# Attention behind the recurrent mixer, and the first tile's sort behind the middle attention

## The chip, the core and the metric

One core of one Trainium2 chip runs the whole program. The metric is the device time of one execution in microseconds; the time before is 3634.22 us, the median of 3 runs (3633.6 to 3636.48). Engines: PE (TensorE, matmul), DVE (VectorE), ACT (ScalarE), POOL (GpSimd), SP (SyncE, which here only issues DMAs). Each takes its instructions in order.

## The reference

One layer of a diffusion backbone on 1024 latent and 256 context tokens of width 1024:

```
hl, hc = rmsnorm(x) * (1 + scale) + shift          # scale and shift from c, c_ctx
r, k, v, w, a, g | q, k, v | b, c, x = split(h @ w_in)
y = concat(rwkv7(r, k, v, w, a, g),                 # two directions, 4 heads, state carried along T
           neighbourhood_attention(q, k, v, ctx),   # 8 heads, window 8 rows x 16 columns, plus 256 context keys
           b * conv3(c * x))
x = x + g1 * (y @ w_out)
h2 = rmsnorm(x) * (1 + scale2) + shift2
q = h2 @ q_w                                        # 8 heads, two halves
idx, gates = softmax(top16 of sums of the top16 of q . sub_keys)
x = x + g2 * sum_k gates[k] * gelu(u[idx[k]] . h2) * v[idx[k]]
out = rmsnorm(x) * final_g
```

All of it is float32 to the outside; a large product is made of three products of a high and a low part (`mm3`, lines 159 to 161), after a cast of each operand to its high part on ScalarE and a subtraction for the low one.

## The kernel before, in words

Stages, by the time in the profiled execution:

- **Projections and mixer (to about 766 us).** `proj` makes 128 output features for a block of 256 or 512 tokens: weights loaded by SP, cast on ACT (L207), low part on POOL (L209), 24 products into a PSUM bank (`pj`), copied out and stored to DRAM. The mixer (`batch(step, d)`) handles 4 chunks of 64 tokens in direction d. It has a long chain: loads, `wr` products, tanh and exponentials on ACT, scans on DVE, products `p1`, `p2`, `tr`, `lkv` for each of two pairs of heads, a substitution of 15 steps on DVE (L575 to L577, result `XT`), products `x0`, `lp`, `lt`, `lx` twice, `x12`, `pr`, then 4 chunks of state steps (`mc`, `yc`, copy `M` on ACT). The second direction to reach a chunk adds both outputs, normalises them on DVE (`y`, `yd`, L674), turns them with the product `yo` and stores them to `d_y`.
- **Fillers.** `fill(BESIDE)` is called six times in a batch and takes work from the generator `others()` until the amount owed is used up. `others()` holds the remaining projections, the convolution (`conv`, on DVE, its tiles `cu`, `cz`, `cs` loaded and stored by SP), then the first attention (query tiles 0 and 1) and the middle attention (2 to 5).
- **Attention.** `attend` runs per head: loads of keys, queries and values from DRAM (`kd`, `qd`, `vN`), casts (`kh`, `qs` on ACT, `kl` on POOL, low half of `qs` on DVE, L728), then for each query tile the score products `pw` and `pc`, maxima on DVE, exponentials on ACT, transposes `pt`, copies, the product `po` and the scaling `yn` (L776). A pair "head, query tile" is called a tile of attention below; the first attention has 16, the middle one 32. The argument `tags` names the PSUM banks of `pw`, `pt`, `po` and `pc`: ra has 3 banks, rb 2, ch 1, pj 2.
- **Group 0 (tokens 0 to 255).** `group(0)`: 192 output products (`o`) of the mixers' results `d_y`, norm and transposes (`s2`, `xt`), 16 query products of 24 matmuls (`q`), each copied on ACT (`qh`, L923), multiplied with keys (`sc`, L926), copied (`so`) and searched on DVE (`top_keys`). `topk(0)` sorts the first tile on DVE, in two halves; its first step is a cast on ACT (`tf`, L952).
- **Group 1 (tokens 256 to 767)** follows, with row gathers on POOL and their sums on DVE beside it, then the dense expert stage, with which the program goes on to its end. The last attention (tiles 6 and 7) and group 2 run inside it.

What sets the order: the kernel is written in program order, and a scheduler orders each engine's instructions ahead of time by what was emitted first and what it takes to be ready then. On the chip each engine keeps this order, so that an instruction that waits holds all behind it. Tiles are recycled: a tile waits until the last reader of the one that had its space is done.

Of the kernel before, what the change touches and what calls it, by code (L numbers as in the profile page):

```python
# [40 lines left out]
PACE = dict(g0=5, g1=(40,), u=450)  # L41
# [7 lines left out]
EASED = (1, 5, 7)  # L49
LAST = (7, 0, 8, 1, 9, 2, 3, 4, 5, 6)  # L50
HP = (600, 500)
BESIDE = 1.4


@with_exitstack
def hybrid_kernel(ctx: ExitStack, tc: tile.TileContext, A: dict, out: bass.AP, dbg=None):
    nc = tc.nc
# [6 lines left out]
    def pool(name, bufs=1, side="left"):  # L64
        return tc.tile_pool(name=name, bufs=bufs, side=side, reuse_waits="tile")
# [106 lines left out]
    def drain(gen):  # L172
        for _ in gen:
            pass
# [17 lines left out]
    def load_h(t0, n, i):  # L192
        new_h((t0, n), i)
        for k2 in range(KD // 2):
            hf = WT[0].tile([P, 2, 512], F32, tag=WT[1][0], name=f"hf{k2}_{t0}{i}", bufs=NWB)[:, :, :n]
            nc.sync.dma_start(hf, d_h[:, 2 * k2:2 * k2 + 2, t0:t0 + n])
            for j in range(2):
                split_h(2 * k2 + j, hf[:, j, :], n)
# [178 lines left out]
    def conv_inputs(blk):  # L377
        for i in range(2):
            zc = stg(f"zc{i}{blk[0]}")
            yield proj(23 + i, blk, lambda ps, t0, n, zc=zc: nc.scalar.copy(zc, ps))  # L380

            def uev(ps, t0, n, i=i, zc=zc):
                ev = nc.vector.tensor_mul(zc, ps, zc)
                nc.sync.dma_start(d_u[:, i, t0 - TC:t0 - TC + n], zc)
                return ev

            yield proj(25 + i, blk, uev)
            yield proj(21 + i, blk, spill(d_zb[:, i, :], TC))

    def head_inputs(blk, na=0):  # L390
        for i in range(4):
            more_ada(na)
            yield proj(13 + i, blk, spill(d_kn[:, i, :]))
            yield proj(17 + i, blk, spill_tok(d_vn, i * P))
            if blk[0]:
                more_ada(na)
                yield proj(9 + i, blk, spill(d_q[:, i, :], TC, scale=0.125))
# [65 lines left out]
    def batch(step, d):  # L463
# [14 lines left out]
        for h in range(2):  # L478
# [83 lines left out]
            for u in range(4):  # L562
# [4 lines left out]
                        rx=rx, krd=krd, vS=vS, tot=tots, gt=gt)  # L567
            fill(BESIDE)

# [15 lines left out]
        nc.scalar.copy(X, v8(ps))  # L585
        fill(BESIDE)

        for l in range(2):
# [13 lines left out]
            nc.vector.tensor_add(XT, v8(ps), XT)  # L602
            fill(BESIDE)
        for h in range(2):
# [7 lines left out]
        for h in range(2):  # L612
# [7 lines left out]
            s["pr"] = pr  # L620
        fill(BESIDE)

# [76 lines left out]
                nc.sync.dma_start(d_y[:, 6 + i, t0:t1], s_)  # L699


    def attend(na, qbs, w0, w1, tags, nbuf):


        q0, nq, nk = qbs[0] * P, len(qbs) * P, TC + w1 - w0
        yns = [na.tile([P, 512], F32, tag=f"yn{i}", name=f"yn{qb}", bufs=1) for i, qb in enumerate(qbs)]
        ns = TC + (640 if any(4 <= 2 * qb <= 10 for qb in qbs) else 512)
        for hd in range(8):
            f, half = divmod(hd, 2)
            if not half:  # L710
                vN, fs = na.tile([P, nk // P, P], F32, tag="vN", name=f"vN{f}{q0}", bufs=2), slice(f * P, (f + 1) * P)
# [79 lines left out]
    def others():  # L791

        for blk, na, i in ((TBLK[2], 2, None), (TBLK[1], 1, 1), (TBLK[0], 2, 1)):
            if i is not None:
                load_h(*blk, i)
            for _ in itertools.chain(head_inputs(blk, na), conv_inputs(blk) if blk[0] else ()):
                yield blk[1] / 512
        st_w.close()
        nc.vector.tensor_add(modT[:, 16:, 0], modT[:, 16:, 0], ab[:, 16:])
        conv(0, 256)  # L800
        conv(256, TL)
        with pool("na", 2, "right") as na:
            for _ in attend(na, range(0, 2), 0, 512, ("ra", "pj", "pj", "ra"), (3, 2, 1, 2, 1)):
                yield 0.6
        with pool("nb1", 1, "right") as na:
            for _ in attend(na, range(2, 6), 0, 1024, ("ra", "pj", "pj", "ra"), (3, 2, 1, 1, 1)):
                yield 0.6

    rest, owed = others(), [None]

    def fill(n):

        if owed[0] is not None:
            owed[0] += n
            while owed[0] > 0:
                owed[0] -= next(rest, 100.0)
# [15 lines left out]

    st_k = ExitStack()
    tk = st_k.enter_context(pool("tk", 1, "right"))
    st_i = ExitStack()
    ip = st_i.enter_context(pool("ip"))
    idx = ip.tile([P, 8, P], I32, name="idx")
# [318 lines left out]
    def advance(n):  # L1156

        while done[0] < n:
            done[0] += 1
            next(gat, None)  # L1160
# [21 lines left out]
        gbase[0] = g0 + ng  # L1182

    with pool("tp") as tp_:
        for i, _ in enumerate(group(0, tp_, nc.vector)):
            if i == 15:
                drain(topk(0, 0, 4))
                advance(PACE["g0"])
        drain(topk(0, 4, 4))
    hb2 = st_u.enter_context(pool("hb2"))  # L1190
    hd_["h2"] = [hb2.tile([P, KD, TD], F32R, name=n_) for n_ in ("h2h", "h2l")]
    h2h, h2l = hd_["h2"]
# [7 lines left out]

    def last_tiles():
        with pool("nb", 2, "right") as na:
            yield from attend(na, range(6, 8), 512, 1024, ("ra", "rb", "ch", "ra"), (2, 2, 1, 2, 2))
        yield from range(REST[0])
        with pool("tp2", 1, "right") as tp_:
            for i, ev in enumerate(group(2, tp_, nc.vector)):
                if i % 2:
                    yield ev
                if i == 7:
                    yield from range(REST[1])  # L1210
# [15 lines left out]
    def operands(g, j):  # L1226
# [16 lines left out]
        vs.append((vh, vl))  # L1243

    rest, opened, onehot, gdone = last_tiles(), True, None, 0
    st_g = ExitStack()
    for e in range(P):
# [202 lines left out]
```

## Time and profile before

| | us |
|---|---|
| median of 3 runs | 3634.2 |
| profiled execution | 3638.1 |
| its span | 3636.1 |
| last projection's end | 766 |
| last product of the mixer (`yo`) | 1063 |
| first output product of group 0 | 1078 |
| last query product of group 0 | 1219 |
| first output product of group 1 | 1236 |

Reading: the page gives each engine's busy share; the times of the table are from the timeline of PE. A stage is a stretch between two of them, and busy time over length tells which engine fills it. The idle time of an engine says little before one knows what ended it.

### The profile page before, as it was taken

To read this page: it belongs to the slowest core of one execution; us is meant where nothing else is said; L and a number is where in the kernel's file an instruction comes from. 1 tells how busy PE (TensorE), PEld (TensorE's weight loads), DVE (VectorE), ACT (ScalarE), POOL (GpSimd) and SP (SyncE) were. 2 spreads that over 40 slices of the span, in tenths; PEclk is the share of its full clock that TensorE was granted. 3 is DMA by queue.
4 is the path that set the end of the run, shared out by engine and by line. 5 is a ranking of instruction groups with operands and counts; after the bars stand their busy time and mean duration, and the time that the engine had idled before them with its cause. 6 is when DMAs were issued, how large, how long until landed. Compare 5 with 4: busy or idle time off the path is not lost. (4 is left out here: it accounts for less than half of the span.)

```text
span 3636.1 us, 62360 instructions
## 1 busy us (share of the span) xinstructions
PE 3270.1 (90%) x23447; PEld 2910.8 (80%) x23447; DVE 2796.9 (77%) x6131; ACT 1515.4 (42%) x2921; POOL 1357.7 (37%) x1052
## 2 busy tenths in 40 slices
PE   7788899858798679899899999999987999999997
PEld 6566778657688558889899999999976788888885
DVE  6654444546666859898899999998868888888888
ACT  3543333225455333364335766666522333323322
POOL 3332233211110132554334335455544444444433
PEclk9899999979799889999999999999998999999998
DMA  7434444353345446999888779999899999999996
GB/s 253 138 100 140 140 133 138 110 149 89 87 117 167 156 154 205 333 311 346 271 294 284 266 277 360 340 369 368 325 354 371 361 350 349 357 350 342 354 348 236
DMA packets 404718, 926.39 MB, mean 255 GB/s; under 512 B 45504, under 2 KB 182080, under 8 KB 398784
## 3 DMA queue, kind: packets, MB, share of 16 engines
q1 hardware_dynamic: 246976, 406.71, 34.7%
q0 software_dynamic: 111920, 407.95, 31.0%
q10 hardware_dynamic: 45520, 107.76, 7.7%
q8 instruction: 184, 3.01, 0.3%
q14 instruction: 118, 0.97, 0.1%
HBM read 800.64 MB, written 121.63 MB: 254 GB/s over the span
## 5 line engine op out<-in xcount | busy, mean ns | idle before, releaser
L1119 POOL DMA_INDIRECT ru<-in_peer_u_dram,idx x384 | 516.5, 1345 | 700.9 <-ACT dqs L1353 155.1
L1119 POOL DMA_INDIRECT rv<-in_peer_v_dram,idx x384 | 502.1, 1307 | 663.7 <-ACT dqs L1353 186.4
L1147 DVE SCALAR_TENSOR_TENSOR acc<-rv,gw,acc 128x1024 f32<-128x1024 f32 x381 | 488.4, 1282 | 30.1 <-DMA rv<-in_peer_v_dram,idx 25.5
L1136 DVE CUSTOM_DVE_ANT_0 ru<-ru,h 128x1024 f32<-128x1024 f32 x384 | 463.6, 1223 | 42.2 <-DMA ru<-in_peer_u_dram,idx 41.9
L160 PE MATMUL dp<-dvls,dwhs 128*128 128x512 f32 x896 | 348.3, 391 | 0.0
L161 PE MATMUL dp<-dvhs,dwls 128*128 128x512 f32 x896 | 346.5, 391 | 0.0
L209 POOL TENSOR_TENSOR wl<-w,wh 128x1024 fp32r<-128x1024 f32 x68 | 165.3, 2433 | 385.1 <-ACT wh L207 372.5
L159 PE MATMUL dp<-dvhs,dwhs 128*128 128x512 f32 x896 | 247.5, 394 | 0.1
L159 PE MATMUL pj<-hbh,wh 128*128 128x512 f32 (+1 forms) x544 | 219.4, 404 | 26.0 <-ACT wh L207 12.2
L160 PE MATMUL pj<-hbl,wh 128*128 128x512 f32 (+1 forms) x544 | 213.5, 393 | 3.7 <-POOL hbl L190 3.7
L1268 ACT ACTIVATE ge<-ds 128x256 f32<-128x256 f32 (+1 forms) x256 | 110.7, 433 | 250.0 <-PE ds L161 235.1
L161 PE MATMUL pj<-hbh,wl 128*128 128x512 f32 (+1 forms) x544 | 211.6, 389 | 2.8 <-POOL wl L209 2.8
L159 PEld LDWEIGHTS dp<-dvhs,dwhs 128*128 128x128 f32 x896 | 170.8, 191 | 36.1 <-ACT dvhs L1234 0.6
L160 PEld LDWEIGHTS dp<-dvls,dwhs 128*128 128x128 f32 x896 | 169.7, 189 | 35.6
L161 PEld LDWEIGHTS dp<-dvhs,dwls 128*128 128x128 f32 x896 | 169.5, 189 | 35.6
L1238 ACT CAST dwhs<-dws 128x640 fp32r<-128x640 f32 x128 | 91.9, 731 | 238.0 <-DVE dws L1237 209.4
L159 PE MATMUL dq<-dvhs,dwhs 128*128 128x512 f32 x384 | 151.6, 395 | 33.0 <-ACT dvhs L1234 26.5
L1234 ACT CAST dvhs<-dvs 128x1024 fp32r<-128x1024 f32 x128 | 134.0, 1051 | 90.8 <-DMA dvs<-in_peer_v_dram 90.7
L207 ACT CAST wh<-w 128x1024 fp32r<-128x1024 f32 x68 | 71.1, 1046 | 233.8 <-PE pj L160 151.9
L1353 ACT COPY dqs<-dq 128x512 f32<-128x512 f32 x90 | 52.8, 587 | 277.1 <-PE dq L161 277.1
L1051 PE MATMUL gm<-oa,ob 128*128 128x128 f32 x1280 | 159.1, 277 | 4.0 <-DVE oa L1038 3.3
L1235 DVE TENSOR_TENSOR dvls<-dvs,dvhs 128x1024 fp32r<-128x1024 f32 x128 | 156.0, 1219 | 8.3 <-ACT dvhs L1234 8.1
(1980 smaller groups left out, 9975.1 us busy)
## 6 DMA issues: line engine op xcount, KB each, us to landing
du<-in_peer_ut_dram SPq DMA_DIRECT2D x128, 512.0 KB, 6.2
dvs<-in_peer_v_dram SPq DMA_DIRECT2D x128, 512.0 KB, 6.9
d_ge<-ge ACTq DMA_DIRECT2D x128, 320.0 KB, 5.5
d_g<-gt ACTq DMA_DIRECT2D x40, 1024.0 KB, 9.8
dgs<-d_g SPq DMA_DIRECT2D x32, 1280.0 KB, 8.9
dws<-d_ge SPq DMA_DIRECT2D x128, 320.0 KB, 8.9
w<-in_w_in_dram SPq DMA_DIRECT2D x68, 512.0 KB, 3.7
wq<-in_q_w_dram SPq DMA_DIRECT2D x48, 512.0 KB, 4.2
```

The lines of the kernel that those rows point to most:

```text
L159: nc.tensor.matmul(ps, lh_, rh_, start=start, stop=False)
L160: nc.tensor.matmul(ps, lh_, rl_, start=False, stop=False)
L161: nc.tensor.matmul(ps, ll_, rh_, start=False, stop=stop)
L209: WE[0].tensor_tensor(wl, w, wh.bitcast(F32), op=OP.subtract)
L1051: nc.tensor.matmul(ps[:, t * P:(t + 1) * P], ob[:, q + t], oa[:, q + t], start=True, stop=True)
L1119: paced(nc.gpsimd.indirect_dma_start(out=r, out_offset=None, in_=A[tab], in_offset=bass.IndirectOffsetOnAxis(ap=idx[:, tt, s:s + 1], axis=0)))
L1136: yield from rows("peer_u", tt, lambda s, u: nc.vector.tensor_tensor_reduce(u, u, h2, 1.0, 0.0, OP.mult, OP.add, act[:, s:s + 1]))
L1147: nc.vector.scalar_tensor_tensor(acc, v, w[:, s:s + 1], acc, op0=OP.mult, op1=OP.add)
L1234: nc.scalar.copy(vh, v)
L1235: sv = nc.vector.tensor_tensor(vl, v, vh.bitcast(F32), op=OP.subtract)
L1238: nc.scalar.copy(wh, wt)
L1268: ev = nc.scalar.activation(ge[:, t0:t0 + n], ps, AF.Gelu_apprx_tanh)
```

## The change

Four edits. `BESIDE` goes from 1.4 to 1.2. Both attentions leave `others()`: the first is emitted behind the last batch of the mixer, with all four roles on the bank tag pj for heads 0 to 3 and ra, pj, ch, ra from head 4 on (so `tags` becomes a function of the head); the middle one, now with ch instead of pj for `po`, is emitted behind group 0. The sort of tile 0 is one piece instead of two halves, behind the middle attention; the first five steps of the gathers (`advance`) follow it as before. Computation and data are the same.

```diff
-BESIDE = 1.4
+BESIDE = 1.2
...
-    def attend(na, qbs, w0, w1, tags, nbuf):
+    def attend(na, qbs, w0, w1, tags_, nbuf):
...
         for hd in range(8):
+            tags = tags_(hd)
...
         conv(256, TL)
-        with pool("na", 2, "right") as na:
-            for _ in attend(na, range(0, 2), 0, 512, ("ra", "pj", "pj", "ra"), (3, 2, 1, 2, 1)):
-                yield 0.6
-        with pool("nb1", 1, "right") as na:
-            for _ in attend(na, range(2, 6), 0, 1024, ("ra", "pj", "pj", "ra"), (3, 2, 1, 1, 1)):
-                yield 0.6
...
     tk = st_k.enter_context(pool("tk", 1, "right"))
+    with pool("na", 2, "right") as na:
+        drain(attend(na, range(0, 2), 0, 512, lambda hd: ("pj",) * 4 if hd < 4 else ("ra", "pj", "ch", "ra"), (3, 2, 1, 2, 1)))
...
     with pool("tp") as tp_:
-        for i, _ in enumerate(group(0, tp_, nc.vector)):
-            if i == 15:
-                drain(topk(0, 0, 4))
-                advance(PACE["g0"])
-        drain(topk(0, 4, 4))
+        drain(group(0, tp_, nc.vector))
+    with pool("nb1", 1, "right") as na:
+        drain(attend(na, range(2, 6), 0, 1024, lambda hd: ("ra", "pj", "ch", "ra"), (3, 2, 1, 1, 1)))
+    drain(topk(0))
+    advance(PACE["g0"])
```

Three places in the order show what this moves. First PE behind the last projection, before: `mc_31` and `yo02`, `yo12` belong to batch (3, 1), `pw00`, `pc00` to head 0, query tile 0.

```order
L461 MATMUL mc_31_7632<-M_332_7709,pr_311_7488 64x64 x2
L461 MATMUL yo02_7780<-cst_729,yd_310_7778 64x64 x8
L461 MATMUL yo12_7792<-cst_729,yd_311_7790 64x64 x8
L749 MATMUL pw00_7420<-kh00_7402,qs00_7404 128x256
L753 MATMUL pc00_7423<-kh00_7402,qs00_7404 128x256
L749 MATMUL pw01_7503<-kh00_7402,qs00_7404 128x256
```

The same place now: `lp_401` belongs to batch (4, 0), `bo11`, `wr43` and `p1_43` to the second pair of heads of batch (4, 1).

```order
L461 MATMUL bo11_8339<-cst2_95,rb_411_8338 64x2 x6
L504 MATMUL wr43_8350<-lwt41_8210,wup_731 128x256
L505 MATMUL wr43_8350<-lwt41_8210,aup_732 128x256
L461 MATMUL lp_401_7970<-X_40_7723,EL_400_7275 64x64 x8
L461 MATMUL lp_401_7970<-X_40_7723,EL_401_7550 64x64 x8
L750 MATMUL pw00_8837<-kh00_8819,qs00_8821 128x256
L751 MATMUL pw00_8837<-kl00_8829,qs00_8821 128x256
L754 MATMUL pc00_8840<-kh00_8819,qs00_8821 128x256
L755 MATMUL pc00_8840<-kl00_8829,qs00_8821 128x256
L754 MATMUL pc00_8840<-kh00_8819,qs00_8821 128x256
L755 MATMUL pc00_8840<-kl00_8829,qs00_8821 128x256
L461 MATMUL p1_43_8381<-krd3_785,bb_410_8377 64x128 x8
```

Behind the last projection stood the end of batch (3, 1) and whole tiles of attention; now the products of the last two batches stand there with single tiles between. By the order, 1652 small products of the mixer lie behind the last projection before, and 1118 now, and 4 tiles of attention finish before the mixer's last `yo` does.

Second, PE between two query products of group 0, before, with `sc05` waiting for the copy of `q05`:

```order
L159 MATMUL q05_11781<-hh0_11470,wq05h_11777 128x256
L160 MATMUL q05_11781<-hl0_11471,wq05h_11777 128x256
L161 MATMUL q05_11781<-hh0_11470,wq05l_11779 128x256
L926 MATMUL sc05_11810<-keys05_11806,qh05_11808 128x128 x2
L159 MATMUL q06_11831<-hh0_11470,wq06h_11827 128x256
```

and now, with parts of head 2 and 3 of the middle attention (query tiles 2 to 4):

```order
L159 MATMUL q05_10345<-hh0_10034,wq05h_10341 128x256
L160 MATMUL q05_10345<-hl0_10035,wq05h_10341 128x256
L161 MATMUL q05_10345<-hh0_10034,wq05l_10343 128x256
L776 MATMUL po22_11304<-vN1256_11254,pT22_11292 128x64 x3
L770 MATMUL pt234_11338<-cst2_95,s23_11313 128x128 x3
L770 MATMUL pt240_11371<-cst2_95,s24_11352 128x128 x4
L750 MATMUL pw32_11449<-kh3256_11431,qs3256_11433 128x384
L776 MATMUL po23_11343<-vN1256_11254,pT23_11331 128x64 x4
L923 MATMUL sc05_10374<-keys05_10370,qh05_10372 128x128 x2
L159 MATMUL q06_10395<-hh0_10034,wq06h_10391 128x256
```

Five tiles of the middle attention now end before the first query product, 12 between the query products and 15 behind the last; before, all 32 ended ahead of the query products.

Third, ACT at the start of group 1, before (`tf0_4` is the sort's second half, `h2h` takes group 1's inputs `yk`):

```order
L928 COPY so015_12385<-sc015_12382 128x256
L1062 CAST wo11h_12539<-wo11_12537 128x1024
L1062 CAST wo12h_12577<-wo12_12575 128x1024
L952 CAST tf0_4_12397<-ti0_11562 128x128
L1196 CAST h2h_12459<-ht_12464 128x8x128
L875 CAST h2h_12459<-yk12_12470 128x512
```

and now, where `pT75` and `yt32560` are the last of the middle attention:

```order
L772 COPY pT75_12296<-pt754_12303 128x384
L785 COPY yt32560_12322<-yt32560_12317 128x512
L786 DMA d_y_70<-yt32560_12322 128x512
L1193 CAST h2h_12434<-ht_12439 128x8x128
L872 CAST h2h_12434<-yk12_12445 128x512
```

The sort's casts on ACT now stand among the middle attention's instructions, ahead of these rows. From the middle of group 1 on, the order of every engine is the same in both programs; on PE these are the last 11,362 rows.

## Rows read from the trace of the kernel before

**Rows 1.** Page, busy time of each engine in the span.
```profile
PE 3270.1 (90%) x23447; PEld 2910.8 (80%) x23447; DVE 2796.9 (77%) x6131; ACT 1515.4 (42%) x2921; POOL 1357.7 (37%) x1052
```
**Rows 2.** Stages: us, then busy PE, PEld, DVE, ACT, POOL; clock, DMA share, GB/s.
```profile
700.00:766.00 66.00, 41.83 (x517) 38.85 (x513) 39.92 (x114) 16.41 (x30) 21.70 (x12) 0.79 0.55 165
766.00:806.00 40.00, 14.33 (x294) 12.37 (x292) 20.74 (x46) 6.09 (x15) 1.80 (x1) 0.69 0.48 134
806.00:913.00 107.00, 94.36 (x1048) 82.12 (x1048) 62.43 (x249) 52.72 (x141) 16.71 (x15) 0.86 0.38 109
913.00:1064.00 151.00, 124.82 (x1289) 111.00 (x1290) 98.68 (x343) 72.02 (x171) 21.62 (x43) 0.84 0.28 77
...
1078.00:1122.00 44.00, 43.02 (x362) 42.63 (x362) 31.16 (x83) 28.29 (x60) 2.93 (x1) 0.99 0.49 149
1122.00:1144.00 22.00, 19.14 (x116) 18.04 (x116) 12.25 (x32) 17.65 (x35) 5.09 (x8) 0.75 0.28 98
1144.00:1219.00 75.00, 60.12 (x464) 56.94 (x465) 63.10 (x297) 26.65 (x50) 3.82 (x5) 0.98 0.55 176
1219.00:1236.00 17.00, 1.30 (x8) 0.90 (x7) 15.88 (x76) 4.89 (x8) 2.26 (x2) 0.58 0.59 204
...
1431.00:3636.00 2205.00, 2089.62 (x12378) 1913.71 (x12376) 1939.46 (x3482) 967.08 (x1846) 1003.08 (x750) 0.98 0.92 328
```
**Rows 3.** Waits of PE at 766 to 807: us in total, times, longest.
```profile
PE yo L461 <- DVE yd L674: 20.2, 1, 20.2
```
**Rows 4.** Timeline of SP: start us, us, DMA issued.
```profile
764.99 0.33 SPq L692 DMA_DIRECT2D cu<-d_u  x1
...
795.80 0.43 SPq L712 DMA_DIRECT2D vN<-d_vn  x1
```
**Rows 5.** Small products of the mixer (L461), PE busy by stretch; clock, DMA.
```profile
500.00:766.00 266.00, 79.71 (x2048) 0.93 0.45 136
766.00:1064.00 298.00, 81.95 (x1644) 0.83 0.34 96
```
**Rows 6.** Timeline of PE, batch (4, 0) and the wait behind it.
```profile
881.24 1.15 PE L461 MATMUL x<-cst,XT 64*64 64x64 f32 x32
...
912.52 0.33 PE L461 MATMUL yc<-M,pr 64*64 64x64 f32 x4
922.98 0.69 PE L749 MATMUL pw<-kh,qs 128*128 128x384 f32 x1 [10.13 <-DVE qs L728]
923.46 0.41 PE L753 MATMUL pc<-kh,qs 128*128 128x256 f32 x1
```
**Rows 7.** Timeline of DVE, first and last of batch (4, 1)'s substitution.
```profile
960.08 0.18 DVE L575 STREAM_SHUFFLE yb<-Y 128x16 f32<-128x16 f32 x1
...
981.32 0.69 DVE L579 TENSOR_TENSOR XT<-Y,cst 128x512 f32<-128x512 f32 x1
```
**Rows 8.** Tiles of attention ended (L776), by stretch; the count is (x).
```profile
806.00:908.00 102.00, 4.47 (x16) 0.85 0.36 103
...
1025.00:1080.00 55.00, 3.10 (x11) 0.84 0.49 141
1080.00:1145.00 65.00, 2.54 (x9) 0.91 0.41 130
```
**Rows 9.** Output products of group 0 (tile o): PE, PEld, DVE busy.
```profile
1080.00:1145.00 65.00, 26.92 (x190) 24.22 (x189) 3.82 (x8) 0.91 0.41 130
```
**Rows 10.** Waits of PE at 1144 to 1240.
```profile
PE sc L926 <- ACT qh L923: 15.0, 16, 2.1
```
**Rows 11.** Timelines of SP, PE and ACT around group 0 and group 1.
```profile
1063.61 0.37 SPq L679 DMA_DIRECT2D d_y<-gs  x1
...
1078.45 0.36 PE L159 MATMUL o<-ah,wo00h 128*128 128x256 f32 x1
...
1233.91 0.30 ACT L952 CAST tf<-ti 128x128 bf16<-128x128 uint32 x1 [2.80 <-DVE ti L944]
...
1235.72 0.80 PE L159 MATMUL o<-h2h,wo10h 128*128 128x512 f32 x1 [15.19 <-ACT h2h L875]
```

More of the change, by code (lines that the diff above doesn't have):

```diff
@@ L1202, in last_tiles @@
         with pool("nb", 2, "right") as na:
-            yield from attend(na, range(6, 8), 512, 1024, ("ra", "rb", "ch", "ra"), (2, 2, 1, 2, 2))
+            yield from attend(na, range(6, 8), 512, 1024, lambda hd: ("ra", "rb", "ch", "ra"), (2, 2, 1, 2, 2))
         yield from range(REST[0])
```

## Prediction

> **What bounds the kernel now.** I read the page first, then the busy time by stage, then PE's waits in the stages where PE stands idle, then the stretch of each wait in order of time. The page has PE at 90% of the span and DVE at 77% [rows 1]. The stages show that the loss is not spread evenly [rows 2]: in the last 2205 us PE is busy for 2089.6 us at a granted clock of 0.98, and that stage is as long as PE makes it. The change does not reach it: on PE the last 11,362 rows of the order are the same in both programs, from the middle of group 1 on. What can move is the time at which group 1 starts, 1235.7 us [rows 11], and everything behind it shifts with it. I forecast that start.
>
> Four places before it are poor. At 700 to 766 us, where the last projections run beside the mixer, PE is idle for 24.2 us of 66. At 766 to 806 us PE works 14.3 of 40 [rows 2], because the mixer's output product (yo) waits 20.2 us for DVE [rows 3]; SyncE, in order, hangs in the convolution's loads and stores from 765.0 to 795.8 us before the first loads of attention can go [rows 4]. At 1144 to 1219 us the query products of group 0 run alone, 60.1 of 75 us, and PE waits 15.0 us in 16 pieces for the copy of each product [rows 2, 10]. At 1219 to 1236 us PE does 1.3 us of work while DVE is busy for 15.9 of 17 [rows 2]: the second half of the first tile's sort, and ScalarE's cast of that half (tf) stands in front of the casts of group 1, which PE waits for 15.2 us [rows 11].
>
> **The change part by part.** No arithmetic is added or taken away. The share of projection work owed at each gap of the mixer falls from 1.4 to 1.2, attention leaves the generator that fills the gaps, the first attention goes behind the mixer (its heads 0 to 3 on the two banks pj alone), the middle attention behind group 0, and the sort of tile 0 behind that. I build the new start of group 1 from the last projection.
>
> Last projection: now 766 us. With fewer projections per gap more of the mixer's small products go ahead of it: behind the last projection the order has 1118 of them where it had 1652, so 534 move, at 79.7 us / 2048 = 0.039 us each [rows 5], 21 us. Of the 24.2 us idle at 700 to 766 us I let them take 9; bounds are 0 and 21. That gives 766 + 21 - 9 = 778.
>
> Rest of the mixer: what remains begins at the first product of batch (4, 0) after its substitution. The same stretch of the same batch takes 881.2 to 912.8 us now, 32 us [rows 6]. The products that feed the second half of batch (4, 1) stand behind the second correction (lp) of batch (4, 0), about half way through it, 16 us in (an estimate). From there (4, 1) needs its substitution on DVE, 960.1 to 982.0 us, 22 us [rows 7], and the same 32 us: 16 + 22 + 32 = 70. Four tiles of attention stand between; half of their PE work (3.9 us a tile, below) I let the mixer's waits take, the other half, 8, is added. ScalarE has the first head's cast (kh) ahead of the tanh of that second half, so it waits for head 0's loads; the loads now stand between the convolution's pieces on SyncE instead of behind all four, and I price the wait at a quarter of the 30.8 us [rows 4], 8 us, bounds 0 and 31. Queued behind this cast are the mixer's own copies on ScalarE, and behind them PE. Sum 86, at 864 us.
>
> First attention: the order puts 4 of its 16 tiles beside the mixer and 12 behind it. 16 tiles took 102 us beside the mixer, 6.4 each; 11 of the middle ones took 55 us with hardly any other work, 5.0 each [rows 8]. I take 5.0, 60 us, up to 924; the two banks of heads 0 to 3 would push towards 6.4 (77 us). Then a store and a load of the head output stand between attention and group 0, with nothing on PE to cover them: from the store at 1063.6 to the first product at 1078.4 us it took 15 us through queues with other work [rows 11]; I take 12. Group 0 output products: 26.9 us [rows 9], in the order nearly alone, 28. Norm and transposes: 22 us now with 4 tiles inside, 24 with 5 [rows 2].
>
> Query products: 60.1 us of PE work [rows 2], with 12 tiles of the middle attention between them. A tile's PE share: at 1078 to 1144 us PE is busy 43.0 + 19.1 us, 26.9 of it output products, so 35 us for 9 tiles, at most 3.9 each [rows 2, 8, 9]. 60.1 + 12 x 3.9 = 107, 110 with some wait; the 15.0 us of small waits are what this work covers. DVE, at 63.1 us in this stage with the sort, has room.
>
> Last 15 tiles with the sort beside them: 5.0 each, and 0.4 for DVE's sort instructions between a tile's own, 81 us; 7.2 (65 us / 9) where they slow each other [rows 8] would be 108. The start of group 1 behind it: its casts follow attention's last copy on ScalarE at once, and seven of eight feature blocks are there already, 3 us; the sort's cast is no longer in front of them.
>
> Sum: 778 + 86 + 60 + 12 + 28 + 24 + 110 + 81 + 3 = 1182, against 1235.7: 54 us earlier. The profiled execution took 3638.1 us (span 3636.1 and 2.0 around it); minus 54 is 3584. It lies 3.9 us above the median of the three runs, 3634.2, so against the median the forecast is 3634.2 - 54 = 3580 us.
>
> The part most open is the mixer's tail, since PE is thinly fed there. PE's clock stands at 0.86 and 0.84 in the stages where mixer and attention share it, 0.69 where PE mostly waits, and 0.98 to 0.99 in the dense stages [rows 2]. After the 10.1 us wait at 922.98 us the products run at the lower of the two levels, 1.2 GHz: 256 columns take 0.41 us there [rows 6]. The Trainium skill (TensorE: Matmul & The Clock Gate, section HAM oscillation — how this bites in real kernels) says that a product loop with waits between its groups keeps falling back to the low rate, which speaks against a tail with little attention; the trace agrees in kind. By that rule the time would be 3637 us (worked out as the third rival, from rows); by the pace of the rows, which I take, 3580.
>
> **The rivals.**
> 1. PE hardly waits. Left after 778 us are 1118 small products at 0.050 (81.95 / 1644 [rows 5]), 48 tiles at 3.9, 26.9 + 60.1 and some 15 of norm work: 345 us, with 15 us for the round trip 1138, 98 us earlier: 3536. For it: 62.2 of 66 us at 1078 to 1144 [rows 2]. Against: the mixer's chain alone needs 70 us for 56 us of work.
> 2. The first heads do not fit beside the mixer, because four steps of a tile share two banks and stand in order behind the mixer's waits: 4 tiles at 6.4 more, 26 us: 3606.
> 3. Order on DVE and PE eats the gain. Sort and attention slow each other (15 tiles at 7.2, +27), and the query products keep their 15 us of waits plus the 12 tiles at 5.0, 135 for 110 (+25): 3632, no change. The clock gives the same end another way: 56 us of mixer and 16 x 3.9 of attention, 118 us at about 0.86, would need 118 x 0.86 / 0.5 = 203 us if all of it ran at 1.2 GHz, 57 more than the 146 allowed: 3637.
> 4. Slower: loads of heads hold the mixer. Both ScalarE and DVE have attention's casts (kh, qs) in front of mixer steps that nothing else can replace; one such wait is 10.1 us [rows 6] and the first one, behind the convolution on SyncE, up to 30.8 [rows 4]. The whole 30.8 (+23) and 10.1 for each of heads 1 to 5 (+50) give 73 us more: 3653. It decides from a mixer tail of about 140 us on, where the 54 us are used up. Against it: head 0's loads now have two convolution pieces fewer before them.
>
> **How the numbers follow.** Forecast 0.52 (its own range 3557 to 3607), PE hardly waiting 0.19, first heads late 0.08, gain eaten 0.11, slower 0.10. A measurement of this kernel can tell 0.2%, 7 us. Faster 0.52 + 0.19 + 0.08 = 0.79; within, 0.11; slower, 0.10. The range reaches to the first rival's floor, within 2 us, and to the middle of no change: 3538 to 3633.
>
> **What would show it.** Right: group 1's first product at 1150 to 1210 us; last projection at 770 to 790; no wait of 20 us at yo; query products spread over about 110 us with attention between and no row of 15 us of sc waits; no wait of 15 us at the start of group 1; the stretch from there to the end unchanged at 2400 us within a few. Wrong: a mixer tail of 130 us or more behind the last projection, tiles at 7 us in the sort's stretch, or a later part that is longer than now because it starts earlier.

## The result: 33 us faster

| | before | changed |
|---|---|---|
| median, us (4 runs each) | 3633.91 (3633.02 to 3636.48) | 3600.84 (3599.58 to 3601.61) |
| span of the profiled execution | 3636.1 | 3597.6 |
| first output product of group 1 | 1235.7 | 1202.6 |
| from there to the end | 2400.4 | 2395.0 |

The ratio is 0.9908, 95% interval 0.9890 to 0.9925: 33 us faster, clear of the interval, where the forecast had 54. The result lies inside the forecast range (3538 to 3633). The gain lies where the sum looked for it: in the profiled executions group 1 starts 33.1 us earlier, and the part behind it is 5.4 us shorter.

The page of the changed kernel, against [rows 1]: the same 23447 products with 12 us less busy time, in a shorter span.

```profile
PE 3257.7 (91%) x23447; PEld 2906.9 (81%) x23447; DVE 2803.5 (78%) x6117; ACT 1514.4 (42%) x2918; POOL 1364.3 (38%) x1052
```

Stages of the changed kernel, with cuts at its own milestones: us, then busy PE, PEld, DVE, ACT, POOL; clock, DMA share, GB/s. The last projection ends at 790, the mixer's last `yo` at 904, the first attention at 963.5, the output products of group 0 at 994; the query products run from 1025 to 1126, and the middle attention ends at 1199.4.

```profile
500.00:700.00 200.00, 176.61 (x2193) 146.48 (x2188) 103.01 (x310) 60.78 (x116) 58.11 (x41) 0.94 0.41 120
700.00:790.00 90.00, 72.17 (x854) 64.22 (x852) 56.10 (x138) 30.05 (x65) 33.41 (x27) 0.89 0.48 143
790.00:806.00 16.00, 11.45 (x279) 10.28 (x278) 10.59 (x27) 4.81 (x11) 1.50 (x1) 0.95 0.54 138
806.00:864.00 58.00, 37.30 (x570) 34.63 (x570) 41.37 (x132) 13.30 (x32) 6.12 (x5) 0.68 0.33 94
864.00:904.00 40.00, 33.71 (x417) 29.11 (x414) 21.46 (x65) 13.14 (x36) 4.77 (x35) 0.77 0.25 76
904.00:964.00 60.00, 44.84 (x299) 40.93 (x299) 29.08 (x108) 30.72 (x81) 5.73 (x3) 0.83 0.48 149
964.00:994.00 30.00, 26.20 (x179) 24.68 (x180) 16.66 (x28) 12.13 (x20) 2.97 (x1) 0.89 0.79 212
994.00:1025.00 31.00, 24.75 (x175) 20.55 (x174) 21.91 (x70) 26.29 (x57) 7.23 (x8) 1.00 0.43 127
1025.00:1126.00 101.00, 95.63 (x794) 93.87 (x793) 86.74 (x360) 62.61 (x136) 13.17 (x6) 0.98 0.52 157
1126.00:1199.40 73.40, 58.27 (x389) 54.59 (x388) 60.57 (x268) 37.02 (x91) 10.64 (x7) 0.82 0.38 128
1199.40:1202.50 3.10, 0.48 (x1) 0.18 (x1) 1.67 (x3) 2.15 (x4) 0.00 (x0) 0.50 0.25 96
```

Compare with [rows 2]: the 75 us of query products with PE at 60 are now 101 us with PE at 95.6, and the 17 us with PE at 1.3 are now 3.1. In their place stands a new thin stretch, 806 to 864 us, with PE at 37.3 of 58 and the clock at 0.68. Up to group 1 PE now stands idle for 200 us (1202.5 less 1002.5 busy), before for 223 (1235.7 less 1013.0); the other 10.5 us of the earlier start are the same 10336 products in less busy time. Only the first part repeats. A second profiled execution of the change (below) has 200.5 us of idle time again, but 1012.9 us of busy time, as much as the kernel before. So what these traces show of the change is some 22 us of idle time filled.

Tiles of attention ended in the changed kernel (L777 is the `yn` that was L776 in [rows 8]): us, DVE busy, count; clock, DMA.

```profile
806.00:904.00 98.00, 1.41 (x5) 0.71 0.30 87
904.00:964.00 60.00, 3.12 (x11) 0.83 0.48 149
1025.00:1126.00 101.00, 3.57 (x13) 0.98 0.52 157
1126.00:1199.40 73.40, 4.15 (x15) 0.82 0.38 128
```

Five tiles ended beside the mixer, 11 in the 60 us behind it; of the middle attention 13 between the query products and 15 behind them (the other 4 ended ahead of the query products): what the order showed, to within a tile.

Waits of PE from the norm to the last query product (total, times, longest). The 15.0 us for `qh` of [rows 10] are gone, and what is left is small:

```profile
PE pw L750 <- DVE qs L729: 5.6, 4, 2.6
PE po L776 <- DVE yn L777: 3.0, 5, 1.0
```

Timeline of PE at the start of group 1, against the 15.19 us of [rows 11]:

```profile
1199.44 0.48 PE L783 MATMUL yt<-cst,yn 128*128 128x128 f32 x1 [0.55 <-DVE yn L777]
1202.55 0.80 PE L159 MATMUL o<-h2h,wo10h 128*128 128x512 f32 x1 [2.64 <-ACT h2h L872]
```

And the part from the first product of group 1 to the end, first before, then changed (columns as in the stages):

```profile
1235.70:3636.10 2400.40, 2257.19 (x13111) 2046.68 (x13111) 2087.51 (x3995) 1028.94 (x1936) 1056.47 (x791) 0.97 0.89 316
```

```profile
1202.60:3597.60 2395.00, 2255.13 (x13111) 2047.37 (x13111) 2076.30 (x3953) 1027.66 (x1933) 1062.32 (x791) 0.97 0.89 317
```

### The profile page after: what moved, and what is told of

The parts are those of the page before. It is cut to its first block, busy times and chain, and to the rows that moved or that the text cites. A ratio compares the mean times of both kernels' runs of the same rounds, so it can differ in the third digit from the quotient of the medians.

```text
span 3597.6 us, 62347 instructions
## 1 busy us (share of the span) xinstructions
PE 3257.7 (91%) x23447; PEld 2906.9 (81%) x23447; DVE 2803.5 (78%) x6117; ACT 1514.4 (42%) x2918; POOL 1364.3 (38%) x1052
## 5 line engine op out<-in xcount | busy, mean ns | idle before, releaser
L727 POOL TENSOR_TENSOR kl<-kd,kh 128x768 fp32r<-128x768 f32 (+1 forms) x24 | 55.0, 2290 | 319.2 <-ACT kh L725 293.0
## 6 DMA issues: line engine op xcount, KB each, us to landing
d_g<-gt ACTq DMA_DIRECT2D x40, 1024.0 KB, 10.5
```

## The experiments

The theory was that of the prediction: PE's idle places are filled by attention that stood elsewhere. Open were which of the four edits carries the gain, and why 21 us of the forecast did not come. Times of different chips scatter (the kernel before had medians of 3631.6 to 3635.9 on them, single runs from 3623 to 3651), so I read ratios to the kernel before on the same chip, and from the traces the start of group 1 and the length of what follows, apart. Each kernel has one trace; two traces of the change differ by 10.8 us in the start of group 1 (1202.6 and 1213.4, below), so that smaller differences of single starts prove little.

**The sort alone.** The kernel before with the sort in one piece behind group 0.

```diff
-        for i, _ in enumerate(group(0, tp_, nc.vector)):
-            if i == 15:
-                drain(topk(0, 0, 4))
-                advance(PACE["g0"])
-        drain(topk(0, 4, 4))
+        drain(group(0, tp_, nc.vector))
+    drain(topk(0))
+    advance(PACE["g0"])
```

> The kernel before with the sort of tile 0 in one piece behind group 0 and nothing else changed. Theory A (most of the 33 us lies in group 0: query products covered by the middle attention, and the sort's cast no longer in front of group 1's casts): only the 15.2 us wait at the start of group 1 can go, and the sort has no attention beside it, so 0 to 10 us faster, 3624 to 3634. Theory B (most of it lies where the first attention takes over from the projections, 766 to 806 us): no change, 3630 to 3638.

Measured: 3633.1 us, ratio 1.0002 (0.9985 to 1.0018). Group 1 starts 7 us earlier, at 1228.6, and the part behind takes 8 us more (2408.8). In the total, the sort's place alone is worth nothing. The time lies in the ranges of both theories, so it does not tell them apart.

**Middle attention and sort, the first attention left as a filler** (BESIDE 1.4).

```diff
-        with pool("nb1", 1, "right") as na:
-            for _ in attend(na, range(2, 6), 0, 1024, ("ra", "pj", "pj", "ra"), (3, 2, 1, 1, 1)):
-                yield 0.6
...
+        drain(group(0, tp_, nc.vector))
+    with pool("nb1", 1, "right") as na:
+        drain(attend(na, range(2, 6), 0, 1024, ("ra", "pj", "ch", "ra"), (3, 2, 1, 1, 1)))
+    drain(topk(0))
+    advance(PACE["g0"])
```

The lines taken out of `others()` come first; the loop of group 0 with the halved sort goes as in the experiment above.

> The kernel before with the middle attention (po on the bank ch) and the whole sort behind group 0; the first attention stays a filler of the mixer and the share of projections stays 1.4. Theory A: the 15.0 us of waits of the key products and the 15.2 us at group 1's start go, 20 to 30 us faster, 3604 to 3614. Theory B: at most 8 us faster, 3626 to 3634, since the attention taken out of the mixer's gaps leaves PE idle there.

Measured: 3624.4 us, ratio 0.9987 (0.9977 to 0.9997), a few us: theory B by its price, at most 8; the expected 20 to 30 of theory A did not come. PE's wait for `yo` of [rows 3] is still there, and the mixer's last `yo` comes at 977 instead of 904. PE's wait, then the stages 765.4 to 806 and 806 to 977 of this kernel:

```profile
PE yo L461 <- DVE yd L674: 20.3, 1, 20.3
```

```profile
765.40:806.00 40.60, 14.50 (x292) 12.67 (x292) 21.42 (x47) 6.50 (x16) 1.80 (x1) 0.69 0.46 134
806.00:977.00 171.00, 130.60 (x1765) 116.31 (x1764) 102.54 (x387) 64.51 (x169) 20.65 (x52) 0.81 0.23 67
```

From the last projection (765.4) to the last `yo` it takes 211.5 us with the first attention in the gaps. With the first attention behind the mixer, and BESIDE 1.4 here too (the next experiment), mixer and first attention together take 190.4, from 773.4 to 963.8. The difference, 21 us, is about the wait for `yo` above. The output products start at 987.4, in the change at 914.7. The query products are filled much as in the change (1055.7 to 1153), and group 1 starts at 1231.4, 28 us later than in the next experiment. So the middle attention and the sort pay little without the first attention behind the mixer, which lets the mixer, and with it group 0, end early enough. Whether moving the first attention alone would pay was not run.

**BESIDE back at 1.4** in the changed kernel.

```diff
-BESIDE = 1.2
+BESIDE = 1.4
```

> The changed kernel with 1.4 instead of 1.2. Theory A1: 1.2 costs PE time between 500 and 700 us (idle 23.4 us there, 11.5 before), so 1.4 gives some of it back and the tail of the mixer grows by less: 3589 to 3600. Rival: 1.2 was needed, because every mixer product that lies behind the last projection runs in a thin stretch: with about a batch more of it 10 to 25 us slower than the change, 3611 to 3626.

Measured: 3600.83 us, ratio 0.9918 (0.9899 to 0.9937): the same as the change, just above the range of theory A1 and 10 us below the rival's. The last projection ends at 773.4 instead of 790.1, and the tail behind it takes 126.9 instead of 113.9; group 1 starts at 1203.0 against 1202.6. The views below, the stage 500 to 700 us of the kernel before, then PE's wait for the substitution there, before (in this kernel it is the same row) and in the change, show what 1.2 costs ahead of 790: the substitution's end (`XT`) has less projection work over it.

```profile
500.00:700.00 200.00, 188.54 (x2232) 156.47 (x2231) 88.74 (x239) 67.46 (x133) 68.49 (x54) 0.97 0.42 126
```

```profile
PE x L461 <- DVE XT L579: 3.9, 1, 3.9
```

```profile
PE x L461 <- DVE XT L579: 16.0, 3, 7.8
```

In the change PE is busy for 176.6 us of this stage, 11.9 less than the 188.5 before; the wait for `XT` alone is 12.1 us longer. With 1.4 it is 3.9 again and PE busy 187.6.

**What fills the mixer's tail: the convolution.** Both convolutions behind the first attention.

```diff
-        conv(0, 256)
-        conv(256, TL)
...
+    conv(0, 256)
+    conv(256, TL)
```

> The changed kernel with the convolution emitted behind the first attention instead of behind the last projection. Theory C (the mixer's tail took 114 us instead of 86 because DVE and SyncE are held by the convolution's single-buffered loads and stores, 2.6 + 4.0 us of waits and 10 us of work on DVE, and head 0's loads stand between them): the tail shrinks by 10 to 20 us, 3581 to 3592. Rival (the tail is the mixer's own chain and the casts of the heads in front of it): 3597 to 3606.

Measured: 3623.2 us, ratio 0.9973 (0.9957 to 0.9989), slower than the change and outside both ranges. In the trace the tail is 102.4 us, 11.5 shorter as theory C had it (last `yo` 9 us earlier), and the first attention ends 17 us earlier, at 946.2. PE's 7.8 us of waiting for the mask `pm`, the longest wait of the change's tail (its row stands further down), is not among this kernel's waits: the convolution on DVE had caused it. But the output products then wait for the convolution's own outputs, as PE's row at 900 to 990 us shows (8.6 us before `ah`), and group 1 starts at 1209.3:

```profile
PE o L159 <- ACT ah L872: 8.6, 3, 4.4
```

The larger part of the loss is behind the start of group 1, where this kernel takes 2415.6 us (see "The part behind").

**The tail without attention.** The first attention is left out; zeros are stored for its outputs.

```diff
-    with pool("na", 2, "right") as na:
-        drain(attend(na, range(0, 2), 0, 512, ...))
+    with pool("na", 1, "right") as na:
+        zt = na.tile([P, 4, 256], F32, name="zt")
+        nc.gpsimd.memset(zt, 0.0)
+        nc.sync.dma_start(d_y[:, 2:6, 0:256], zt)
```

> The changed kernel without the first attention: its 16 tiles are left out and zeros are stored for their outputs, so the mixer's tail runs without them (the middle attention follows group 0 as before). Read is the stretch from the last projection to the last yo, 114 us in the changed kernel, forecast 86. Theory A (attention's casts and tiles in front of the mixer's steps are what made it long): 70 to 80 us, yo at 855 to 870. Theory B (the mixer's own chain is that long when nothing covers it, through the convolution on DVE and the low clock): 100 to 114 us.

Measured (one run, 3538 us): from the last projection, 789.4, to the last `yo`, 874.6, 85.2 us, between the two theories. The stage, and PE's two largest waits in it:

```profile
789.40:874.60 85.20, 52.51 (x1122) 49.09 (x1122) 54.91 (x164) 14.13 (x33) 3.28 (x35) 0.74 0.18 56
```

```profile
PE lt L461 <- DVE pm L593: 12.1, 2, 9.0
PE yo L461 <- DVE yd L674: 9.7, 2, 8.2
```

So the mixer alone, with the convolution on DVE beside it, needs 85 us where I had 70, and attention adds 29 where I had 16. The timelines of DVE and PE in this kernel show where the 85 us lie:

```profile
806.79 0.62 DVE L695 TENSOR_SCALAR cs<-cu,cvw 128x768 f32<-128x768 f32 x1 [3.71 <-DMA cu<-d_u]
809.44 0.69 DVE L521 TENSOR_TENSOR_SCAN pe<-de,d 128x260 f32<-128x260 f32 x1
...
811.83 0.69 DVE L593 TENSOR_TENSOR pm<-lp,cst 128x512 f32<-128x512 f32 x1
812.57 1.97 PE L461 MATMUL lt<-XT,pm 64*64 64x64 f32 x32 [8.96 <-DVE pm L593]
...
820.82 0.17 DVE L576 TENSOR_TENSOR yb<-yb,E 128x8 f32<-128x8 f32 x1
...
833.52 0.69 DVE L579 TENSOR_TENSOR XT<-Y,cst 128x512 f32<-128x512 f32 x1
...
863.31 0.33 PE L461 MATMUL yc<-M,pr 64*64 64x64 f32 x4
871.89 1.12 PE L461 MATMUL yo<-cst,yd 64*64 64x64 f32 x16 [8.24 <-DVE yd L674]
```

Up to the substitution of batch (4, 1) it takes 31.4 us (the sum has 16), the substitution 13.4 (22), from there to the last `yc` 29.4 (32), and the closing normalisation with its product `yo` 11.0, for which the sum has nothing. In the first part DVE stands in a convolution step that waits 3.71 us for its load; the scan `pe` behind it starts at 809.44, though ScalarE had its input `de` done at 800.6, and PE waits 8.96 us for `pm`. PE's wait of 3.1 us for the tile `X` just ahead of that stands behind another convolution step in the same way. Without these two waits, 12.1 us, the tail would be some 73 us (an estimate); the mixer without the convolution as well was not run.

The whole first attention costs 74 us at the start of group 1 (1128.5 against 1202.6).

**The banks of heads 0 to 3.**

```diff
-lambda hd: ("pj",) * 4 if hd < 4 else ("ra", "pj", "ch", "ra")
+lambda hd: ("ra", "pj", "ch", "ra")
```

> The changed kernel with the usual banks (ra, pj, ch, ra) for heads 0 to 3 of the first attention too. Theory A (two banks for four steps slow these tiles): the first attention ends some 10 us sooner, group 1 starts at 1190 to 1195, 3589 to 3593. Theory B (ra and ch belong to the mixer's products, and attention in them makes the mixer wait for banks): the last yo comes 5 to 20 us later than 904, the total is 3603 to 3620.

Measured: 3614.8 us, ratio 0.9937 (0.9913 to 0.9962). Up to group 1 it is near theory A, but by another way: no tile ends before the last `yo`, the tail is 98.8 us, the first attention ends at 950.1 and group 1 starts at 1196.3, 6 us before the change, which one execution each cannot tell from nothing. Banks and places in the order changed together, so this does not show which of them shortens the tail. The tail of this kernel:

```profile
792.50:891.30 98.80, 61.85 (x1166) 56.85 (x1166) 66.27 (x195) 23.96 (x57) 10.59 (x39) 0.76 0.34 92
```

The total is not shorter (the two ratios' intervals overlap), because the part behind takes 2419.4 us. It lies in theory B's range, but not by theory B, whose later `yo` did not come.

**The middle attention ahead of group 0**, directly behind the first one; the sort stays.

```diff
     with pool("na", 2, "right") as na:
         drain(attend(na, range(0, 2), ...))
+    with pool("nb1", 1, "right") as na:
+        drain(attend(na, range(2, 6), 0, 1024, ...))
...
         drain(group(0, tp_, nc.vector))
-    with pool("nb1", 1, "right") as na:
-        drain(attend(na, range(2, 6), 0, 1024, ...))
```

> The changed kernel with the middle attention directly behind the first one, ahead of group 0, instead of behind it; the sort stays in one piece behind group 0. Theory A (the gain comes from tiles lying between and behind the query products): the query products run alone again (75 us, some 15 us of it waits) and the sort is bare again (17 us), group 1 starts at 1235 to 1250, 3633 to 3648. Theory B (PE's work is what fills the time, in whatever order): the tiles fill the mixer's tail, the round trip and the norm instead, group 1 starts within 8 us of 1203, 3595 to 3609.

Measured: 3595.3 us, ratio 0.9883 (0.9859 to 0.9906), the same as the change within the intervals. Theory A's times do not come, but its cause was not put to the test: emitted earlier, the attention still lies between the query products (22 tiles end there, 10 ahead of them), because these wait for the norm. Stages from the first attention's end to the first query product, through them, and to group 1:

```profile
963.60:1051.90 88.30, 70.55 (x508) 68.39 (x509) 56.46 (x152) 55.82 (x119) 17.79 (x12) 0.83 0.58 164
1051.90:1177.60 125.70, 121.78 (x1024) 118.60 (x1022) 100.98 (x438) 77.36 (x176) 11.70 (x4) 1.00 0.43 137
1177.60:1186.20 8.60, 1.23 (x8) 0.87 (x7) 6.60 (x45) 4.34 (x8) 0.00 (x0) 0.73 0.31 103
```

PE is busy for 121.8 of the 125.7 us in the middle row, the tiles behind the query products are gone, and group 1 starts at 1186.2, 16 us before the change and earlier than theory B allowed. PE's idle time up to there is 200.7 us, as in the change: the 16 us are less busy time (985.5 us), and why is open.

**The sort back inside group 0**, the rest as in the change (the diff is the first one, reversed).

> The changed kernel with the sort put back into group 0 in two halves. Theory A (once attention follows group 0, the sort has cover wherever it stands): both halves still lie beside the middle attention, nothing bare is left in front of group 1; 0 to 4 us slower than the change, 3601 to 3605. Theory B (DVE is in order, so a sort in front of the middle attention's maxima holds PE): 15.9 us of DVE work come back into the path, 3613 to 3617, with waits of PE on DVE of some 10 us at the first tiles behind the last query product.

Measured: 3627.4 us, ratio 0.9981 (0.9967 to 0.9996), slower than the change and above both ranges. Group 1 starts 7 us later (1209.6); from the last query product to there it takes 82.3 us where the change has 76.3. PE's two waits behind the query products that grew:

```profile
PE po L776 <- DVE yn L777: 7.0, 3, 3.5
PE pw L750 <- DVE qs L729: 5.9, 3, 3.2
```

`yn` and `qs` are steps of DVE, which takes the sort in order ahead of attention here: 7.0 us where the change has 5.2, and 5.9 where it has no such row. That is theory B at about half its size; the larger part of the loss is again behind the start of group 1 (2414.9).

**The part behind.** In six of the runs above it took 2408 to 2419 us instead of 2389 to 2400. Comparing orders, in the long ones only the last 1,650 to 2,360 rows of PE are the change's, in the short ones mostly over 11,000 (with BESIDE 1.4, 3,080). Three kernels to tell this from a slow chip: the change once more, unedited; BESIDE 1.25 (with which the later order differs); and the usual banks with BESIDE 1.35 (with which it is the change's).

> The changed kernel once more, beside the two kernels below on one chip. In the earlier experiments the part behind the start of group 1 took 2389 to 2395 us where the later order of PE is (nearly) the change's, and 2413 to 2419 where it is another. Theory A (the order of that part decides): this one again 2393 to 2399, total 3598 to 3605. Theory B (the chips of those runs were slower): 2405 to 2420 here too, total 3610 to 3625.

> The changed kernel with BESIDE 1.25 in place of 1.2, between the change and the 1.4 that was tried and made no difference. Group 1 starts at 1200 to 1205 in either theory. In the order of PE only the last 2233 rows are the change's. Theory A (the order behind decides): that part takes 2408 to 2420, total 3610 to 3625. Theory B (the order behind is worth nothing): 2390 to 2399, total 3595 to 3605.

> The usual banks for heads 0 to 3 once more, now with BESIDE 1.35, with which the last 11,572 rows of PE's order are those of the change. Group 1 starts at 1193 to 1200, as with the usual banks before (1196). Theory A (the order behind decides): that part takes 2390 to 2399, total 3585 to 3598, faster than the change. Theory B (the usual banks themselves slow what follows, 2419 before): total 3610 to 3620.

Measured on one chip, where before had 3635.88: the change 3598.1 (0.9887, 0.9865 to 0.9909), BESIDE 1.25 3608.8 (0.9914, 0.9894 to 0.9934), usual banks with 1.35 3595.5 (0.9891, 0.9871 to 0.9912). The part from group 1 to the end in these three, in this order:

```profile
1213.40:3607.20 2393.80, 2255.01 (x13111) 2046.01 (x13111) 2077.51 (x3953) 1028.29 (x1933) 1061.80 (x791) 0.97 0.89 317
```

```profile
1201.40:3610.50 2409.10, 2260.82 (x13111) 2051.52 (x13111) 2077.66 (x3953) 1024.55 (x1931) 1054.87 (x791) 0.97 0.89 315
```

```profile
1201.50:3591.80 2390.30, 2253.37 (x13111) 2046.66 (x13111) 2077.39 (x3953) 1029.36 (x1933) 1063.14 (x791) 0.97 0.90 317
```

2393.8, 2409.1 and 2390.3: each as theory A had it, on one chip. The totals are less sharp: 3608.8 lies 1 us below theory A's range, and the intervals of the three ratios overlap. Group 1 of the usual banks with 1.35 starts at 1201.5, not at the 1193 to 1200 expected. All profiled executions together:

| kernel | last PE rows in the change's order | group 1 starts | to the end |
|---|---|---|---|
| before | 11,362 | 1235.7 | 2400.4 |
| change, two chips | all | 1202.6, 1213.4 | 2395.0, 2393.8 |
| BESIDE 1.4 | 3,080 | 1203.0 | 2393.9 |
| middle attention and sort | 11,560 | 1231.4 | 2389.2 |
| usual banks, 1.35 | 11,570 | 1201.5 | 2390.3 |
| sort alone | 2,360 | 1228.6 | 2408.8 |
| no first attention | 2,250 | 1128.5 | 2407.9 |
| BESIDE 1.25 | 2,230 | 1201.4 | 2409.1 |
| both attentions ahead | 2,360 | 1186.2 | 2413.1 |
| sort in group 0 | 1,650 | 1209.6 | 2414.9 |
| both ahead, usual banks (next) | 2,230 | 1181.5 | 2415.1 |
| convolution late | 2,360 | 1209.3 | 2415.6 |
| usual banks | 2,250 | 1196.3 | 2419.4 |

The scheduler places the expert stage's products anew when something ahead of it shifts, and most of the orders that it then finds are 13 to 24 us longer than the change's; that with BESIDE 1.4, which differs over some 8,000 rows, is not. So the length goes with the order and not with the chip, but which rows make the difference is not settled: in the long ones PE's busy time there rises by 5 to 14 us and its idle time by 1 to 14, spread over many small waits. One caution from the repeated change: in its profiled execution (3609.3, the longest of four, 3594.2 to 3609.3) the last projection ended at 804 instead of 790, with about the same tail, 115.9 against 113.9.

**The two edits that start group 1 earlier, together**: both attentions ahead of group 0, usual banks for all heads.

> Both attentions ahead of group 0 and the usual banks for all heads: the two edits that made group 1 start earlier, together. Additive theory: group 1 at 1180 (1186 less 6); the order behind is another than the change's, so 2408 to 2420, total 3590 to 3602. Rival (both gains are the same idle time of PE): group 1 at 1186 to 1196, total 3597 to 3615.

Measured: 3586.9 us (3579.8 to 3598.8), ratio 0.9854 (0.9831 to 0.9876); the change on the same chip had 0.9887 (0.9865 to 0.9909). It is the fastest median of the study, though the two intervals still overlap, and lies below the ranges of both theories. Up to group 1, and from there:

```profile
0.00:1181.50 1181.50, 982.71 (x10337) 849.13 (x10337) 702.78 (x2072) 483.94 (x982) 299.25 (x256) 0.91 0.46 140
1181.50:3596.60 2415.10, 2265.61 (x13111) 2056.64 (x13111) 2112.75 (x4047) 1036.12 (x1941) 1056.06 (x796) 0.97 0.89 315
```

Group 1 starts at 1181.5, as the additive theory said, though one execution cannot tell that from the rival's 1186. PE is busy for 982.7 us instead of 1002.5, and idle for 198.8, no less than in the change. The part behind is one of the long ones; with the change's order there (2395) it would be some 20 us less, an estimate; no kernel here has both.

## Why the prediction was right, and 21 us too low

The mechanism was right: PE's idle time ahead of group 1 gives, and what follows keeps its order and length. It gives 22 us, though, where the sum took 54 from it; where the rest of the 33 us comes from is not settled (see the result). Against the forecast 1182 group 1 starts at 1202.6. Term by term, forecast and measured:

| term | forecast | measured | miss |
|---|---|---|---|
| last projection | 778 | 790 | +12 |
| mixer's tail | 86 | 114 | +28 |
| first attention behind it | 60 | 59.5 | 0 |
| round trip and output products | 40 | 30.5 | -9.5 |
| norm, transposes | 24 | 31 | +7 |
| query products with tiles | 110 | 101 | -9 |
| last tiles with the sort | 81 | 73.4 | -7.6 |
| start of group 1 | 3 | 3.1 | 0 |

Misses of +47 and -26 partly cancel, so that the sum comes nearer than its terms. The first attention's 60 is luck in part: its 59.5 us hold 11 tiles, not 12, and 42 of the 192 output products, which the forecast had all behind it.

- **Last projection.** The sum let the moved products take 9 us of idle time at 700 to 766. Nothing was priced at 500 to 700, where PE now waits 16.0 instead of 3.9 us for the substitution. BESIDE 1.4 showed that this has no net price: what it saves there it loses in the tail.
- **Mixer's tail**, the largest miss. The term for the mixer alone was 70, and the kernel without the first attention needs 85. Two things were put at nothing: the convolution's steps on DVE, which hold the mixer's own steps there while they wait for transfers (9.0 and 3.1 us of PE's waits), and the closing normalisation with `yo` (11.0 us), since the stretch that was taken as a price ends at the last `yc`. The substitution and the stretch behind it were even shorter there than priced. Eight us of kh wait and 8 of shared tiles became 29. Of the change's 114 us 32.1 lie ahead of the substitution (16 and the wait of 8 were priced), 17.8 in it, 47.3 from there to the last `yc` (32 and the tiles' 8) and 16.8 from there to the last `yo` (nothing). With the usual banks, and no tile in it, the tail is 98.8, 15 us less. The timeline of ScalarE, DVE and PE in the changed kernel shows the first part (idle time before in brackets, with what ended it):

```profile
803.59 0.83 ACT L725 CAST kh<-kd 128x768 fp32r<-128x768 f32 x1 [6.09 <-DMA qd<-d_q]
804.63 0.47 ACT L508 ACTIVATE th<-wr,hb 128x256 f32<-128x256 f32 x1
...
810.73 0.62 DVE L695 TENSOR_SCALAR cs<-cu,cvw 128x768 f32<-128x768 f32 x1 [3.96 <-DMA cu<-d_u]
812.32 0.69 DVE L521 TENSOR_TENSOR_SCAN pe<-de,d 128x260 f32<-128x260 f32 x1
...
812.52 0.40 ACT L728 CAST qs<-qd 128x256 fp32r<-128x256 f32 x1 [5.38 <-DMA qd<-d_q]
813.05 0.20 ACT L532 COPY tots<-pe 128x4 f32<-128x4 f32 x1
...
815.44 0.68 DVE L593 TENSOR_TENSOR pm<-lp,cst 128x512 f32<-128x512 f32 x1
816.12 1.97 PE L461 MATMUL p<-krd,bb 64*64 64x128 f32 x16 [7.83 <-DVE pm L593]
```

ScalarE stands 6.09 us in `kh` for the head's loads with the tanh (`th`) of batch (4, 1) behind it, as forecast. What I had missed is DVE: the scan `pe` of the mixer and the product's mask `pm` stand behind a convolution step that waits 3.96 us for its load, and PE waits 7.83 us for `pm`. PE's wait of 3.40 us for `X` before that has a convolution step ahead of it too; the two together, 11.2 us, are about what the late convolution took off the tail (11.5). The second `qs` also waits, 5.38 us, but it is not shown to hold the mixer: the copy `tots` behind it needs `pe`, which DVE ends only at 813.01. The 20.2 us wait of [rows 3] has the same cause in part: there the normalisation of the mixer's output, from 785.1 us on, stands on DVE behind a convolution step that waits 4.81 us for its load.
- **Clock.** The granted clock is 0.68 in the tail's thin stretch, 806 to 864 us, and 0.74 over the tail without attention, between its two levels (1.2 GHz is 0.5). The Trainium skill (TensorE: Matmul & The Clock Gate, section HAM oscillation — how this bites in real kernels) says that waits between groups of products send the loop back to the low rate; the trace agrees in kind. The mixer's small products did not take PE longer than priced, though: 55.4 us for 1116 in the change's tail, 0.050 each, at a mean clock of 0.75, as in [rows 5] at 0.83:

```profile
790.00:904.00 114.00, 55.37 (x1116) 0.75 0.33 94
```

What the clock costs there in the waits of the chain was not isolated.
- **Query products and last tiles** were better than priced: 95.6 us of PE work hold 60 of query products and 13 tiles, 2.7 us each at a clock of 0.98, against 3.9, which was an upper bound from a stage that also held the norm. Sort and attention are not seen to slow each other: 73.4 / 15 = 4.9 us a tile, against 5.0 priced without the sort.
- **Rivals.** Rival 1 (PE hardly waits) has the work right, 345 us, of which 333 are measured from 790 to 1202.5, but PE waits for another 80 us there. Rival 3 fails on both counts: tiles at 4.9, no `qh` waits. Its other form, by the clock, gave 203 us for mixer and first attention where 146 were allowed; they take 173.4, but with small products no longer than priced. Rival 4's wait on ScalarE is there once, 6.1 us, and not for each head; the longer waits came from the convolution on DVE, which it did not name. Rival 2 comes near in its time, 3606, but not by its way: 5 tiles do end beside the mixer, and what the two banks cost is not settled. With the usual ones the first attention ends 13 us earlier, and group 1 starts 6 us earlier, or 1 with BESIDE 1.35.

## What to carry to other kernels

Fill idle places with independent work that is emitted close behind, not in front of, the chain that is short of time; a part alone can be worth next to nothing (sort 0, middle attention and sort a few us) while the whole is worth 33. Price a chain to its very last product, and look on each in-order engine for steps of other work that wait for a load in front of the chain's own steps: here the convolution on DVE, which the change left where it was. When a scheduler writes the order, compare the order of the untouched part before a total is compared: here it was worth 13 to 24 us, about half of what the change gave. And profile one program twice before a difference of 10 us in single traces is explained.

## Not expected of the hardware

Executions of one program on one chip can differ by 15 us (3594.2 to 3609.3). The slowest of them was profiled, and against the change's first trace, from another chip, it was 14 us late at the last projection and 16 at the last `yo`, won 5 back up to group 1, and then kept the same length (2393.8 against 2395.0). Up to group 1 the difference lies wholly in PE's busy time, 1012.9 against 1002.5 us for the same products in the same order, while its idle time was the same to half a us (200.5 and 200.1). Over the other kernels the same products took PE from 982.7 us (the fastest version) to 1013.0 (the kernel before), at mean granted clocks of 0.88 to 0.91; what makes them longer or shorter is open.
